# Two chunk-state products side by side, and products recorded in bundles, in a planned encoder kernel

## The chip, the cores and the metric

The kernel runs on one core of one Trainium2 chip. What is measured is the time of one execution on the device, in microseconds (us). Three runs of the kernel before took 2340.8, 2342.04 and 2342.53 us; the median, 2342.04 us, is the time before.

## What is computed

The reference is an encoder of two layers over 512 tokens with 1024 features, all in float32. Each layer has three branches that read the same normed input and are merged by sigmoid gates: an attention over a neighbourhood of rows and columns (16 heads), a dilated attention in three groups of 8 heads with windows of 128, 512 and 2048 tokens, and a state-space branch that runs over the tokens in both directions. After the merge come an output projection and a gated embedding. Most of the work is in the projections `h @ w_in`, 16,432 columns wide.

The change touches the state-space branch in its arithmetic. There the 512 tokens are cut in 4 chunks of 128. Per group of heads and direction the reference computes (shortened):

```python
decay_to_end = jnp.exp(a_cum[..., -1:] - a_cum)
chunk_states = jnp.einsum('bclgn,bghcl,bclghp->cbghpn', bc, decay_to_end, xdt)
def carry_state(state, inp):
    st, dec = inp
    return state * dec[..., None, None] + st, state
_, entering = lax.scan(carry_state, init, (chunk_states, chunk_decay))
y_off = jnp.einsum('bclgn,cbghpn,bghcl->bclghp', cc, entering, jnp.exp(a_cum))
```

`bc` is the same in both directions; the scaled inputs differ. Forward, the states of chunks 0, 1 and 2 are needed (the last one enters no chunk), backward those of 3, 2 and 1.

## The kernel before

The kernel is not written in the order in which it runs. `Emit` calls every operation of both layers on a `Recorder`, which makes a node of each call (`add`, line 222) with its engine, its tiles and its predecessors: nodes that wrote what it reads, and so on. A tile in PSUM counts as one whole: every product into it is behind the one before it. Then `schedule` (line 279) plays the program on a model of the chip and writes out an order for each queue; on the chip every engine works off its own order, and a semaphore wait stands where a tile was written by another engine.

In the model an instruction has a price (`cost`, line 151), a transfer has one too, and results come free for other engines after a fixed latency. An engine that is free takes among the nodes whose inputs are ready the one of lowest rank. The rank is the place in the program, less 300 for the weight splits, less 60 for what reads PSUM. For TensorE each product has a mode: `wide` (float32r, the projections), `full` (4-byte products and transposes), `pair` (4-byte products with 64 output rows, where two heads stand side by side in the array), `half` (64 input rows). TensorE's choice stays in the present mode if, among up to 12 older nodes of other modes, there is one of the present mode within 60 places of the oldest. A change of mode is priced at 45 ns between wide and full and 95 ns otherwise.

Around this the program has these parts. `proj` (line 490) makes one block of 128 output columns: a weight block of 128x1024 is fetched on SP's queue, split by ScalarE into a high part (whi) and by VectorE into a low part (wlo), and 24 float32r products of 512 columns go to a PSUM tile pj (3 buffers). `ssm_pair` (line 800) handles two heads of the state-space branch, 12 times a layer: a convolution, chunk states into tiles sc (2 buffers), a recurrence on VectorE over three states for each direction, decay factors from transfers on GpSimd's queue (af, ab, eb), the product inside a chunk into the tile av (1 buffer), 8 products with heads 0 and 1 in turn, and the product with the entering states (yo, in sc). The dilated branch (`dil_half`, line 911) and the neighbourhood branch (`na_unit`, line 1095) each run scores (`scores`, `dil_pair`, into sc), softmax on VectorE and ScalarE, transposes (`turn`, line 1004, into tr) and the products with the values into av, again head 0 and head 1 in turn: 8 products in a group of the dilated branch with dilation, 16 in the near one and in the neighbourhood branch. `stack` (line 1131) makes high and low halves of queries and keys for the score products. The stages run in the order N0 S0 N1 S1 N2 S2, half of the output product, S3 N3, its other half, the gate, D0 D1 (dilated), and the merges; the planner overlaps neighbours in this order.

Each 4-byte product shows in the trace as two TensorE records, each transpose and each float32r product as one. All operations are recorded at one line (270), so that tiles and not lines tell them apart: pj projections, av products with values, tr transposes, sc scores and states.

Of the kernel before, what the change touches and what calls it, by code (L numbers as in the profile page):

```python
# [119 lines left out]

class Node:
    __slots__ = ("i", "eng", "method", "args", "kw", "tiles", "pred", "succ", "cost", "dma", "table", "fetch", "issue",
                 "npred", "ready", "done", "rank", "split", "drain", "mode")


LATENCY = {"PE": {"PE": 0.0, "*": 197.0}, "ACT": {"ACT": 63.0, "PE": 271.0, "POOL": 159.0, "*": 142.0},
# [1 line left out]
           "POOL": {"POOL": 102.0, "PE": 203.0, "*": 75.0}, "SP": {"*": 0.0}}  # L128
RELEASE = {"tensor": 197.0, "scalar": 271.0, "vector": 287.0, "gpsimd": 203.0}
QUEUE = {"sync": "SP", "scalar": "ACT", "gpsimd": "POOL", "vector": "DVE", "tensor": "PE"}  # L130


FLEX = {"either": ("vector", "gpsimd")}
# [17 lines left out]
def cost(n, eng):  # L151

    args = list(n.args) + list(n.kw.values())
    lazy = [v for v in args if isinstance(v, Lazy)]
    out = n.kw.get("out", n.kw.get("out_", n.args[0] if n.args else None))
    if not isinstance(out, Lazy):
        out = lazy[0]
    free = 1
    for o, k, s in out.box[1:]:
        free *= k  # L160
    if n.dma:
        return 4.0 * free * out.box[0][1] / 360.0
    if eng == "tensor":
        if n.method == "transpose":
            return 107.0
        if lazy[1].base.dtype == F32R:
            return 111.0 if lazy[1].box[0][1] == 64 else 0.418 * free + 13.5
        if out.box[0][1] <= 64:
            return 54.0 if out.box[0][0] >= 64 else 1.72 * max(free, 64)
        if lazy[1].box[0][1] == 64:  # L170
            return 136.0
        return 1.75 * max(free, 124)
    psum = any(v.base.pool.space == "PSUM" for v in lazy)
    ptr = sum(1 for v in lazy if v.box[1:] and all(k == 1 for o, k, s in v.box[1:]))
    if eng == "scalar":
        return (51 if psum else 93) + 93 * ptr + free / 1.2
    if eng == "vector":
        if n.method == "reciprocal":
            return 64 + 6.27 * free
        if n.method == "tensor_tensor_reduce":  # L180
            ptr = 0
        half = n.method in ("tensor_copy", "tensor_scalar", "memset") and not psum
        return (64 + 61 * ptr + (free / 2 if half else free)) / 0.96
    if n.method == "memset":
        return 60 + free / 1.2
    if n.method == "tensor_copy":
        return 280 + free / 1.2
    if n.method == "tensor_mul" and any(v.box[-1][1] == 1 for v in lazy):
        return 1000.0
    return 160 + 2.08 * free  # L190


class Recorder:
# [28 lines left out]
    def add(self, eng, method, args, kw):  # L222
        n = Node()
        n.i, n.eng, n.method, n.args, n.kw = len(self.nodes), eng, method, args, kw
        n.dma = method == "dma_start"
        n.split = False
        n.drain = eng != "tensor" and any(isinstance(v, Lazy) and v.base.pool.space == "PSUM"
                                          for v in list(args) + list(kw.values()))
        n.fetch = n.dma and isinstance(kw["out"], Lazy) and kw["out"].base.pool.space != "DRAM"
# [32 lines left out]
        self.nodes.append(n)  # L262
        return n

    def emit(self, tc):
        order = self.schedule()
        with tc.manual_schedule():
            for n in order:
                f = lambda v: v.real() if isinstance(v, Lazy) else v
                getattr(getattr(self.real, n.eng), n.method)(*[f(a) for a in n.args],  # L270
                                                             **{k: f(v) for k, v in n.kw.items()})

    EARLY = 300
    DRAIN = 60
    STAY, NEAR = 12, 60
    WINDOW = 2500
    AHEAD = 600

    def schedule(self):
# [16 lines left out]
        self.first, self.placed = first, set()  # L296
        for n in nodes:
            n.npred = len(n.pred)
            n.rank = n.i - (self.EARLY if n.split else self.DRAIN if n.drain else 0)
            n.ready = 0.0  # L300
            for m in n.pred:
                m.succ.append(n)
            for t, wr in n.tiles.items():
                t.left += 1
# [13 lines left out]
        while len(order) < len(nodes):  # L318
# [3 lines left out]
            for q in avail:  # L322
# [50 lines left out]
                else:  # L373
# [2 lines left out]
                        table = n.table  # L376
                        c += 1283.0
                    if q == "tensor":
                        c += 0.0 if n.mode == mode else 45.0 if {n.mode, mode} == {"wide", "full"} else 95.0
                        mode = n.mode  # L380
                    clock[q] = n.done = now + c
                    busy[q] += c
# [50 lines left out]
class Emit:  # L433
# [366 lines left out]
    def ssm_pair(self, p, C, cbf, cbb, Bt):  # L800
# [2 lines left out]
        zz = self.silu2(self.proj("w_in", ZC + 128 * p))  # L803
        xt = self.transpose4(xs)

        ent = []
        for d in range(2):
            r0 = 32 * d + 2 * p
            c0 = d
            cx = self.t((128, 3, 2, 64), nm="cx")  # L810
            nc.vector.tensor_mul(cx, xt[:, c0:c0 + 3].rearrange("p c (h e) -> p c h e", h=2),
                                 self.cfT[:, c0:c0 + 3, r0:r0 + 2].unsqueeze(3).to_broadcast([128, 3, 2, 64]))
            st = self.ps("sc", (128, 3, 128))
            for c in range(3):
                nc.tensor.matmul(st[:, c], Bt[:, c0 + c], cx[:, c].rearrange("p h e -> p (h e)"),
                                 start=True, stop=True)
            E = self.t((128, 3, 128), nm="ent")
            order = (0, 1, 2) if d == 0 else (2, 1, 0)
            nc.scalar.copy(E[:, order[0]], st[:, order[0]])
            for a, b in zip(order, order[1:]):  # L820
                for h in range(2):
                    hs = slice(64 * h, 64 * h + 64)
                    nc.vector.scalar_tensor_tensor(E[:, b, hs], E[:, a, hs],
                                                   self.dec[:, r0 + h, c0 + b:c0 + b + 1],
                                                   st[:, b, hs], ALU.mult, ALU.add)
            ent.append(E)

        zs = []
        for h in range(2):
# [15 lines left out]
            nc.vector.tensor_mul(z, z, af)  # L845
            zs.append(z)
        yd = self.ps("av", (128, 4, 128))
        for c in range(4):
            for h in range(2):
                nc.tensor.matmul(yd[64 * h:64 * h + 64, c], xt[:, c, 64 * h:64 * h + 64], zs[h][:, c],  # L850
                                 start=True, stop=True)
        y = self.t(nm="y")
        nc.vector.scalar_tensor_tensor(y, xs, self.vec(V_DS + p), yd.rearrange("p c l -> p (c l)"),
                                       ALU.mult, ALU.add)
# [56 lines left out]
    def dil_half(self, hf):  # L911
# [8 lines left out]
        for pp in range(2):  # L920
            P = 2 * hf + pp
            for g in range(3):
# [3 lines left out]
                    qs, ks, kl = self.stack(q, k)  # L926
                pts = self.dil_near(qs, ks, kl, st, 2 * pp) if g == 0 else self.dil_pair(g, q, k, st, 2 * pp)
                av = self.ps("av", (128, 4, 128))
                for i in range(4):
                    terms = [((i + c + 3) % 4, i // 2, 2 * (i % 2) + c) for c in range(2)] if g == 0 else [(i, 0, i)]  # L930
                    for c, (t, b, u) in enumerate(terms):
                        for h in range(2):
                            vo = 128 * pp + 64 * h
                            nc.tensor.matmul(av[64 * h:64 * h + 64, i], val(g, t)[:, vo:vo + 64],
                                             pts[h][b][:, u], start=c == 0, stop=c == len(terms) - 1)
                o = self.t(nm="o")
                if g == 0:
                    nc.scalar.copy(o, av.rearrange("p t m -> p (t m)"))
# [54 lines left out]
    def scores(self, pair, q, k, kl):  # L993

        nc = self.nc
        sc = [self.ps("sc", (128, 2, 256)) for _ in range(2)]
        for h in range(2):
            for ii in range(2):
                nc.tensor.matmul(sc[h][:, ii], q(h, pair, ii), k(h, pair, ii), start=ii == 0, stop=False)
            for ii in range(2):  # L1000
                nc.tensor.matmul(sc[h][:, ii], q(h, pair, ii), kl(h, pair, ii), start=False, stop=ii == 1)
        return sc

    def turn(self, p):
        nc = self.nc
        tr = self.ps("tr", (128, 4, 128))
        pv = p.rearrange("p a (c k) -> p (a c) k", k=128) if p.shape[1] == 2 else p
        for c in range(4):
            nc.tensor.transpose(tr[:, c], pv[:, c], self.ident)
        pt = self.t((128, 4, 128), nm="pt")  # L1010
        nc.scalar.copy(pt, tr)
        return pt
# [36 lines left out]
    def dil_pair(self, g, q, k, st, hl):  # L1049
        nc = self.nc  # L1050
        sc = [self.ps("sc", (128, 4, 128)) for _ in range(2)]
        for t in range(4):
            for h in range(2):
                hs = slice(64 * h, 64 * h + 64)
                nc.tensor.matmul(sc[h][:, t], q[hs, t], k[hs, t], start=True, stop=True)
        pts = []
        for h in range(2):
            mx, dn = self.stats(st, g, hl + h)
# [36 lines left out]
    def na_unit(self, u):  # L1095
# [13 lines left out]
        for pp in range(2):  # L1109
# [4 lines left out]
            zz = self.silu2(self.proj("w_in", GA + 128 * P))  # L1114
            pts = self.na_pair(qs, ks, kl, P)
            av = self.ps("av", (128, 4, 128))
            for j in range(4):
                for c in range(2):
                    for h in range(2):
                        vo = 128 * pp + 64 * h  # L1120
                        nc.tensor.matmul(av[64 * h:64 * h + 64, j], V[self.BAND[j] + 16 * c][:, vo:vo + 64],
                                         pts[h][j // 2][:, 2 * (j % 2) + c], start=c == 0, stop=c == 1)
            y = self.t(nm="y")
            nc.vector.tensor_mul(y.rearrange("p (r j c) -> p j r c", j=4, c=16),
                                 av.rearrange("p j (r c) -> p j r c", c=16),
# [5 lines left out]
    def stack(self, qp, kp, scale=1.0, perm=lambda t: t, view=lambda t: t, eng=None):  # L1131
# [5 lines left out]
        qs = [self.t(dtype=F32R, nm="qs") for _ in range(2)]  # L1137
        ks = [self.t(dtype=F32R, nm="ks") for _ in range(2)]
        kl = self.keylow[self.nkey % 2]
        self.nkey += 1  # L1140
        for h in range(2):
            a, b = own[h], own[1 - h]
# [8 lines left out]
        for h in range(2):  # L1151
# [2 lines left out]
                nc.scalar.copy(ks[h][b], kp[a])  # L1154
            else:
                nc.scalar.activation(ks[h][b], kp[a], AF.Copy, scale=scale)
        return qs, ks, kl

    BAND = (0, 8, 24, 32)
# [259 lines left out]
```

## Time and profile before

| | |
|---|---|
| median of three runs | 2342.04 us |
| profiled execution | 2345.19 us |
| its span, first to last instruction | 2342.9 us |
| TensorE, busy | 2282.3 us (97%) |
| VectorE, busy | 1643.4 us (70%) |
| ScalarE, busy | 1112.8 us (47%) |
| GpSimd, busy | 219.1 us (9%) |
| mean granted clock of TensorE | 0.991 |
| moved by transfers | 272.69 MB, 116 GB/s over the span |

A busy time is the union of the spans of an engine's instructions. Matmuls are pipelined: one starts before the one before it has ended, and its end is modelled. What a product costs in a stream is therefore read from the start of one to the start of another, on the timeline.

### The profile page before, as it was taken

Reading aid. Unit: us, or ns where it says so; the run is one execution under the profiler, and the core shown is the slowest. Engines: PE = TensorE matmul, PEld = TensorE weight load, DVE = VectorE, ACT = ScalarE, POOL = GpSimd, SP = SyncE. Lnnn points to the kernel's source line nnn. Section 1 sums busy time; section 2 is a strip of 40 time slices with the busy share of each in tenths; the row PEclk is TensorE's granted clock in tenths of the full one; section 3 lists DMA queues with packets and bytes.
Section 4 is the critical chain, followed back from the end, with each engine's and each line's share of the span. In section 5 each row is a group of like instructions: output and inputs, shape, how many; then the busy total and the mean of one; then the engine's idle time right before and its main releaser. Section 6 shows DMA issues by size and latency. Waiting matters only on the chain. (4 is left out here: it accounts for less than half of the span.)

```text
span 2342.9 us, 32733 instructions
## 1 busy us (share of the span) xinstructions
PE 2282.3 (97%) x12096; PEld 1880.5 (80%) x12096; DVE 1643.4 (70%) x3227; ACT 1112.8 (47%) x2132; POOL 219.1 (9%) x384
## 2 busy tenths in 40 slices
PE   7899999999999999999998999999999999999998
PEld 6688888888887877888877888888789778778888
DVE  6699979796356577635677998797943666665367
ACT  5456455444345456324465463644532554562245
POOL 1401020010000100200013110210100001011000
PEclk8999999999999999999999999999999999999999
DMA  5734262432221321533256333534322213225324
GB/s 217 212 99 152 85 186 77 144 99 91 90 90 64 91 81 64 172 128 112 105 179 185 110 128 106 161 101 133 107 84 99 72 67 106 73 66 171 111 103 135
DMA packets 109326, 272.69 MB, mean 116 GB/s; under 512 B 39360, under 2 KB 41888, under 8 KB 109168
## 3 DMA queue, kind: packets, MB, share of 16 engines
q1 hardware_dynamic: 56464, 189.73, 23.7%
q0 software_dynamic: 50400, 76.69, 11.6%
q10 hardware_dynamic: 2304, 4.20, 0.5%
q8 instruction: 95, 1.56, 0.3%
q14 instruction: 63, 0.52, 0.1%
HBM read 257.08 MB, written 13.21 MB: 115 GB/s over the span
## 5 line engine op out<-in xcount | busy, mean ns | idle before, releaser
L270 ACT CAST whi<-raw 128x1024 fp32r<-128x1024 f32 (+2 forms) x360 | 368.3, 1023 | 696.8 <-PE pj L270 511.4
L270 PE MATMUL pj<-hl,whi 128*128 128x512 f32 x1744 | 693.3, 398 | 2.1 <-DVE hl L270 2.1
L270 PE MATMUL pj<-hh,whi 128*128 128x512 f32 x1744 | 693.0, 397 | 1.5 <-ACT hh L270 1.5
L270 PE MATMUL pj<-hh,wlo 128*128 128x512 f32 x1728 | 687.4, 398 | 0.4 <-DVE wlo L270 0.4
L270 DVE TENSOR_TENSOR wlo<-raw,whi 128x1024 fp32r<-128x1024 f32 (+2 forms) x358 | 426.3, 1191 | 349.4 <-ACT whi L270 345.9
L270 PEld LDWEIGHTS pj<-hl,whi 128*128 128x128 f32 x1744 | 330.3, 189 | 70.7 <-issue 5.7
L270 PEld LDWEIGHTS pj<-hh,whi 128*128 128x128 f32 x1744 | 330.5, 190 | 66.5 <-issue 2.4
L270 PEld LDWEIGHTS pj<-hh,wlo 128*128 128x128 f32 x1728 | 326.2, 189 | 71.2 <-issue 9.3
L270 PE MATMUL pj<-yh,whi 128*128 128x512 f32 (+1 forms) x576 | 211.9, 368 | 0.0
L270 PE MATMUL pj<-yh,wlo 128*128 128x512 f32 (+1 forms) x576 | 211.5, 367 | 0.0
L270 PE MATMUL pj<-yl,whi 128*128 128x512 f32 (+1 forms) x576 | 211.0, 366 | 0.0
L270 PEld LDWEIGHTS pj<-yh,wlo 128*128 128x128 f32 x576 | 108.7, 189 | 18.0 <-issue 0.7
L270 PEld LDWEIGHTS pj<-yh,whi 128*128 128x128 f32 x576 | 108.6, 189 | 17.5 <-issue 0.7
L270 PEld LDWEIGHTS pj<-yl,whi 128*128 128x128 f32 x576 | 108.7, 189 | 17.1
L270 DVE SCALAR_TENSOR_TENSOR cv<-cx,cwh,cv 128x510 f32<-128x510 f32 (+1 forms) x160 | 119.5, 747 | 2.3 <-ACT cv L270 0.3
L270 ACT ACTIVATE p<-p,nm 128x128 f32<-128x128 f32 (+2 forms) x192 | 80.2, 420 | 33.6 <-DVE nm L270 33.6
L270 PE MATMUL pj<-whi,hh 128*128 128x512 f32 (+1 forms) x256 | 88.7, 348 | 2.0 <-ACT v L270 2.0
L270 PE MATMUL pj<-whi,hl 128*128 128x512 f32 (+1 forms) x256 | 87.6, 342 | 0.8 <-DVE hl L270 0.8
L270 PE MATMUL pj<-wlo,hh 128*128 128x512 f32 (+1 forms) x256 | 87.8, 343 | 0.0
L270 ACT ACTIVATE np<-np,nnm 128x256 f32<-128x256 f32 x128 | 63.7, 499 | 48.9 <-DVE nnm L270 48.9
L270 ACT COPY pt<-tr 128x512 f32<-128x512 f32 x128 | 71.2, 579 | 26.3 <-PE tr L270 25.2
L270 POOL DMA_DIRECT2D af<-acd x48 | 28.4, 591 | 483.3 <-DVE y L270 224.5
(215 smaller groups left out, 3577.9 us busy)
## 6 DMA issues: line engine op xcount, KB each, us to landing
raw<-wt SPq DMA_DIRECT2D x322, 512.0 KB, 3.2
nb<-nab POOLq DMA_DIRECT2D x32, 384.0 KB, 5.4
af<-acd POOLq DMA_DIRECT2D x48, 256.0 KB, 4.8
ab<-acd POOLq DMA_DIRECT2D x48, 256.0 KB, 5.5
raw<-wt SPq DMA_DIRECT2D x32, 384.0 KB, 2.9
eb<-ead POOLq DMA_DIRECT2D x48, 192.0 KB, 8.5
vw<-vd POOLq DMA_DIRECT2D x56, 128.0 KB, 5.0
f<-fd POOLq DMA_DIRECT2D x24, 256.0 KB, 11.1
```

The costliest lines, as they stand in the source:

```text
L270: getattr(getattr(self.real, n.eng), n.method)(*[f(a) for a in n.args], **{k: f(v) for k, v in n.kw.items()})
```

## The change

Six things are changed. The states of both directions are made chunk by chunk: the scaled inputs that share a chunk's weights stand side by side (256 columns for chunks 1 and 2, 128 for 0 and 3), in two PSUM tiles that both recurrences read. A new `bundle` puts all predecessors of a group of products in front of the group's first one; it is called for the av groups, the scores, the transposes and the dilated pairs. A change of mode is priced by a table with an entry for each direction. GpSimd's transfers are priced at 1.6 times, broadcasts by `to_broadcast` at 4 times. The nodes of `stack` are ranked 200 places earlier. A 4-byte product is priced as before.

```diff
+CHANGE = {("wide", "full"): 39.0, ("full", "wide"): 0.0, ("pair", "wide"): 202.0, ("wide", "pair"): 78.0,
+          ("full", "pair"): 108.0, ("pair", "full"): 140.0, ("half", "wide"): 187.0, ("wide", "half"): 53.0}
...
     if n.dma:
-        return 4.0 * free * out.box[0][1] / 360.0
+        c = 4.0 * free * out.box[0][1] / 360.0
+        if eng != "gpsimd":
+            return c
+        ops = [m for m, a, k in n.kw["in_"].ops] if isinstance(n.kw["in_"], Lazy) else []
+        return 4.0 * c if "to_broadcast" in ops else 1.6 * c
...
+    def bundle(self, start):
+
+        group = self.nodes[start:]
+        for eng in {n.eng for n in group}:
+            own = [n for n in group if n.eng == eng]
+            for n in own[1:]:
+                for m in n.pred:
+                    if m.i < start:
+                        own[0].pred[m] = True
...
-            n.rank = n.i - (self.EARLY if n.split else self.DRAIN if n.drain else 0)
+            n.rank = n.i - (self.EARLY if n.split else self.STACK if n.stack else self.DRAIN if n.drain else 0)
...
-                        c += 0.0 if n.mode == mode else 45.0 if {n.mode, mode} == {"wide", "full"} else 95.0
+                        c += 0.0 if n.mode == mode else CHANGE.get((mode, n.mode), 100.0)
...
+        r = (2 * p, 32 + 2 * p)
+        own = lambda lo, n, d: self.cfT[:, lo:lo + n, r[d]:r[d] + 2].unsqueeze(3).to_broadcast([128, n, 2, 64])
+        four = lambda t: t.rearrange("p c (h e) -> p c h e", h=2)
+        ca, cb2 = self.t((128, 3, 128), nm="cx"), self.t((128, 3, 128), nm="cx")
+        nc.vector.tensor_mul(four(ca[:, 0:2]), four(xt[:, 0:2]), own(0, 2, 0))
+        nc.vector.tensor_mul(four(ca[:, 2:3]), four(xt[:, 1:2]), own(1, 1, 1))
+        nc.vector.tensor_mul(four(cb2[:, 0:1]), four(xt[:, 2:3]), own(2, 1, 0))
+        nc.vector.tensor_mul(four(cb2[:, 1:3]), four(xt[:, 2:4]), own(2, 2, 1))
+        sa, sb = self.ps("sc", (128, 3, 128)), self.ps("sc", (128, 3, 128))
+        for st, cx, c, lo, hi in ((sa, ca, 0, 0, 1), (sa, ca, 1, 1, 3), (sb, cb2, 2, 0, 2), (sb, cb2, 3, 2, 3)):
+            nc.tensor.matmul(st[:, lo:hi], Bt[:, c], cx[:, lo:hi], start=True, stop=True)
         ent = []
-        for d in range(2):
-            r0 = 32 * d + 2 * p
-            c0 = d
-            cx = self.t((128, 3, 2, 64), nm="cx")
-            nc.vector.tensor_mul(cx, xt[:, c0:c0 + 3].rearrange("p c (h e) -> p c h e", h=2),
-                                 self.cfT[:, c0:c0 + 3, r0:r0 + 2].unsqueeze(3).to_broadcast([128, 3, 2, 64]))
-            st = self.ps("sc", (128, 3, 128))
-            for c in range(3):
-                nc.tensor.matmul(st[:, c], Bt[:, c0 + c], cx[:, c].rearrange("p h e -> p (h e)"),
-                                 start=True, stop=True)
+        for d, steps in enumerate((((0, 0, sa[:, 0]), (1, 1, sa[:, 1]), (2, 2, sb[:, 0])),
+                                   ((2, 3, sb[:, 2]), (1, 2, sb[:, 1]), (0, 1, sa[:, 2])))):
             E = self.t((128, 3, 128), nm="ent")
...
         yd = self.ps("av", (128, 4, 128))
+        mark = len(nc.nodes)
         for c in range(4):
             for h in range(2):
                 nc.tensor.matmul(yd[64 * h:64 * h + 64, c], xt[:, c, 64 * h:64 * h + 64], zs[h][:, c],
                                  start=True, stop=True)
+        nc.bundle(mark)
...
+        mark = len(nc.nodes)
         for c in range(4):
             nc.tensor.transpose(tr[:, c], pv[:, c], self.ident)
+        nc.bundle(mark)
...
+        for n in nc.nodes[mark:]:
+            n.stack = True
         return qs, ks, kl
```

The same two lines `mark` and `bundle` stand around the av products of `dil_half` and `na_unit` and around the score products of `scores` and `dil_pair`. The recurrence steps and the copies of the first states are the same in number and size.

## Rows read from the trace of the kernel before

**Rows 1.** The page: engine busy us, share, instructions; VectorE's tenths in 40 slices.
```profile
PE 2282.3 (97%) x12096; PEld 1880.5 (80%) x12096; DVE 1643.4 (70%) x3227; ACT 1112.8 (47%) x2132; POOL 219.1 (9%) x384
...
DVE  6699979796356577635677998797943666665367
```
**Rows 2.** Timeline of TensorE, long products: start us, duration us, operation, tiles, shape.
```profile
999.62 0.39 PE L270 MATMUL pj<-hl,whi 128*128 128x512 f32 x1
...
1008.91 0.39 PE L270 MATMUL pj<-hh,whi 128*128 128x512 f32 x1
```
**Rows 3.** Timeline of TensorE, a split av group, state-space; last visit of 14.
```profile
167.13 0.40 PE L270 MATMUL pj<-hl,whi 128*128 128x512 f32 x1
167.45 0.43 PE L270 MATMUL av<-z,tT 128*64 128x128 f32 x2
...
168.16 0.40 PE L270 MATMUL pj<-hh,whi 128*128 128x512 f32 x1
...
171.39 0.39 PE L270 MATMUL pj<-hh,wlo 128*128 128x512 f32 x1
171.71 1.09 PE L270 MATMUL av<-z,tT 128*64 128x128 f32 x14
...
173.06 0.40 PE L270 MATMUL pj<-hl,whi 128*128 128x512 f32 x1
...
1680.61 1.09 PE L270 MATMUL av<-z,tT 128*64 128x128 f32 x14
```
**Rows 4.** Timeline of TensorE, unbroken av visits of 16 and of 32 records.
```profile
338.33 0.40 PE L270 MATMUL pj<-hh,whi 128*128 128x512 f32 x1
338.65 1.09 PE L270 MATMUL av<-pt,vw 128*64 128x128 f32 x16
...
340.01 0.39 PE L270 MATMUL pj<-hh,wlo 128*128 128x512 f32 x1
...
559.84 1.97 PE L270 MATMUL av<-pt,vw 128*64 128x128 f32 x32
...
562.08 0.40 PE L270 MATMUL pj<-yl,whi 128*128 128x512 f32 x1
```
**Rows 5.** Timeline of TensorE, dilated part: the first and last av visit of two.
```profile
691.14 0.43 PE L270 MATMUL av<-pt,v 128*64 128x128 f32 x2
...
2085.58 0.43 PE L270 MATMUL av<-pt,v 128*64 128x128 f32 x2 [0.67 <-ACT pt L270]
```
**Rows 6.** Timeline of TensorE, a single softmax transpose between long products.
```profile
705.55 0.40 PE L270 MATMUL pj<-hl,whi 128*128 128x512 f32 x1
705.81 0.33 PE L270 MATMUL tr<-consts,p 128*128 128x128 f32 x1
...
706.21 0.40 PE L270 MATMUL pj<-hh,whi 128*128 128x512 f32 x1
```
**Rows 7.** Timeline of TensorE, chunk states, and products with one column.
```profile
161.94 1.50 PE L270 MATMUL sc<-cx,tT 128*128 128x128 f32 x12
...
163.51 0.40 PE L270 MATMUL pj<-hh,whi 128*128 128x512 f32 x1
...
596.14 0.95 PE L270 MATMUL sc<-consts,sq 128*128 128x1 f32 x8
...
597.28 0.40 PE L270 MATMUL pj<-hh,wlo 128*128 128x512 f32 x1
```
**Rows 8.** VectorE's groups by form: count, then busy us, mean ns, idle before.
```profile
L270 DVE TENSOR_TENSOR cx<-tT,cfT 128x384 f32<-128x384 f32 x48 | 24.5, 551 | 0.0
...
L270 DVE TENSOR_TENSOR gth<-pj,r 128x256 f32<-128x256 f32 x18 | 7.4, 421 | 2.7 <-PE pj L270 2.7
```
**Rows 9.** Waits of TensorE: us in total, times, longest us.
```profile
PE tr L270 <- DVE np L270: 14.0, 2, 7.1
```
**Rows 10.** One slice: length, busy us of PE, PEld, DVE, ACT, POOL, clock, DMA.
```profile
468.60:527.20 58.60, 57.91 (x325) 47.19 (x325) 58.24 (x113) 27.71 (x45) 6.34 (x11) 1.00 0.32 99
```

More of the change, by code (lines that the diff above doesn't have):

```diff
@@ L122 @@
     __slots__ = ("i", "eng", "method", "args", "kw", "tiles", "pred", "succ", "cost", "dma", "table", "fetch", "issue",
-                 "npred", "ready", "done", "rank", "split", "drain", "mode")
+                 "npred", "ready", "done", "rank", "split", "stack", "drain", "mode")
 LATENCY = {"PE": {"PE": 0.0, "*": 197.0}, "ACT": {"ACT": 63.0, "PE": 271.0, "POOL": 159.0, "*": 142.0},
@@ L225, in add @@
         n.dma = method == "dma_start"
-        n.split = False
+        n.split = n.stack = False
         n.drain = eng != "tensor" and any(isinstance(v, Lazy) and v.base.pool.space == "PSUM"
@@ L274 @@
     DRAIN = 60
+    STACK = 200
     STAY, NEAR = 12, 60
@@ L817, in ssm_pair @@
             E = self.t((128, 3, 128), nm="ent")
-            order = (0, 1, 2) if d == 0 else (2, 1, 0)
-            nc.scalar.copy(E[:, order[0]], st[:, order[0]])
-            for a, b in zip(order, order[1:]):
+            nc.scalar.copy(E[:, steps[0][0]], steps[0][2])
+            for (i, _, _), (j, c, st) in zip(steps, steps[1:]):
                 for h in range(2):
                     hs = slice(64 * h, 64 * h + 64)
-                    nc.vector.scalar_tensor_tensor(E[:, b, hs], E[:, a, hs],
-                                                   self.dec[:, r0 + h, c0 + b:c0 + b + 1],
-                                                   st[:, b, hs], ALU.mult, ALU.add)
+                    nc.vector.scalar_tensor_tensor(E[:, j, hs], E[:, i, hs], self.dec[:, r[d] + h, c:c + 1],
+                                                   st[:, hs], ALU.mult, ALU.add)
@@ L996, in scores @@
         sc = [self.ps("sc", (128, 2, 256)) for _ in range(2)]
+        mark = len(nc.nodes)
         for h in range(2):
@@ L1001, in scores @@
                 nc.tensor.matmul(sc[h][:, ii], q(h, pair, ii), kl(h, pair, ii), start=False, stop=ii == 1)
+        nc.bundle(mark)
         return sc
@@ L1007, in turn @@
         pv = p.rearrange("p a (c k) -> p (a c) k", k=128) if p.shape[1] == 2 else p
+        mark = len(nc.nodes)
         for c in range(4):
             nc.tensor.transpose(tr[:, c], pv[:, c], self.ident)
+        nc.bundle(mark)
         pt = self.t((128, 4, 128), nm="pt")
@@ L1051, in dil_pair @@
         sc = [self.ps("sc", (128, 4, 128)) for _ in range(2)]
+        mark = len(nc.nodes)
         for t in range(4):
@@ L1055, in dil_pair @@
                 nc.tensor.matmul(sc[h][:, t], q[hs, t], k[hs, t], start=True, stop=True)
+        nc.bundle(mark)
         pts = []
@@ L1116, in na_unit @@
             av = self.ps("av", (128, 4, 128))
+            mark = len(nc.nodes)
             for j in range(4):
@@ L1122, in na_unit @@
                                          pts[h][j // 2][:, 2 * (j % 2) + c], start=c == 0, stop=c == 1)
+            nc.bundle(mark)
             y = self.t(nm="y")
@@ L1139, in stack @@
         kl = self.keylow[self.nkey % 2]
+        mark = len(nc.nodes)
         self.nkey += 1
```

## The prediction

> **What bounds the kernel now.** I read the page's engine table first: TensorE is busy 2282.3 of 2342.9 us, VectorE 1643.4 [rows 1]. Matmul ends are modelled, so a busy TensorE may still lose time between products; I therefore went to its timeline and measured from start to start. In an undisturbed stream of long products (float32r, 128x512) 41 of them take 1008.91 - 999.62 = 9.29 us, 0.227 us each [rows 2]. Where another kind of product comes between two long ones, I take the time from the start of the last long one before it to the start of the second one after it, less 2 x 0.227 us. That is the true price of the visit, with what the neighbours lose.
>
> A visit of the half-width kind (outputs 64 rows wide, tile av) prices so. Two records, that is one product: 168.16 - 167.13 - 0.454 = 0.576 us. Fourteen records: 173.06 - 171.39 - 0.454 = 1.216 us [rows 3]. Sixteen: 340.01 - 338.33 - 0.454 = 1.226 us. Thirty-two: 562.08 - 559.84 - 0.227 = 2.01 us, with 0.09 us for the entry 2.10 us [rows 4]. So sixteen more records cost 0.88 us, and a visit as such 1.226 - 0.88 = 0.35 us. Fourteen cost what sixteen do: the lone product at the start of a group takes as long as the pair of products (one for each head, side by side) that it is torn from. The reader is to see that a group split into 2 + 14 costs 0.576 us more than a whole one, and ends no sooner after its last input.
>
> And groups are split nearly always. The timeline holds 149 av visits for 64 groups: all 24 of the state-space part stand as 2 + 14 [rows 3]; the dilated part has 32 of 2 and 32 of 14 records for 24 groups [rows 5]; the neighbourhood part has 37 visits (15 of 16 as in [rows 4], 10 of 2, 7 of 14, 3 of 30, 2 of 32) for 16 groups of 32. The planner issues the first product once head 0 is ready, and then goes back to long products.
>
> **The change part by part.** The sum is made against the profiled execution, 2345.19 us (span 2342.9), which lies 3.15 us above the median of 2342.04.
>
> *Bundles on av.* No product is added or taken away. The first product of a group is planned behind all inputs, the others follow in a chain. Visits go from 149 to 64. State-space: 24 x 0.576 = 13.8 us. Dilated groups of 16: 16 x 0.576 = 9.2 us. Dilated groups of 32, now 2, 14, 2, 14: 8 x (2 x 0.576 + 2 x 1.216 - 2.10) = 11.9 us. Neighbourhood: some 43 to 45 us of visits against 16 x 2.10 = 33.6 us, I take 10 us. Together 45 us, from a timeline in which TensorE has hardly any idle time, so it lies on the path. The bound below is that the visits between other kinds are cheaper; at the bare 0.35 us a visit 85 of them make 30 us. Only the groups of 32 end later after their last input, by 0.88 us; their reader (an ACT copy or a VectorE product) has its next user one projection later.
>
> *Bundles on transposes.* The softmax transposes of the dilated part (4 to a group, 64 groups) stand in 144 visits, 96 of them single. A single one costs 706.21 - 705.55 - 0.454 = 0.206 us [rows 6]; in a run a record of this size costs 0.112 us [rows 7]. 80 visits fewer x 0.094 = 7.5 us at most; many single ones sit beside other 4-byte products, where no visit is closed, so I take 5 us, with 0 as the low end. The first three transposes of a group now wait for the fourth exponential, and the copy behind them comes some 0.3 us later; TensorE has long products meanwhile. The bundles on scores and on the dilated pairs change no kind of product: nothing.
>
> *Chunk states.* Per pair 6 products (12 records) become 4, two with 128 and two with 256 columns. Twelve records take 163.51 - 161.94 - 0.227 = 1.343 us, 0.112 each [rows 7]. Records of 256 columns do not occur in this type. One bound: the time is all streaming, then a 256-column record costs 0.219 to 0.224 us and nothing is gained. The other: the time is all weight load, then it costs 0.112 and each pair gains 4 x 0.112 = 0.448 us, 24 pairs 10.75 us. A record with one column costs 0.114 us [rows 7], which allows the second; but the av products have weights 64 columns wide, and two side by side still take 0.88 us / 8 = 0.110 us a record at 128 columns [rows 4], which speaks for streaming. I take 0.5 us. VectorE gets 2 x 0.421 + 2 x 0.29 us (128 columns, by the slope from 256 to 384) in place of 2 x 0.551 us [rows 8], +0.32 us a pair, 7.7 us in all. Both sc buffers are held until both recurrences end, about 1.1 us longer (four steps); scores, cb and the y products of the next step wait for these buffers, and would cost 24 x 1.1 = 26 us if TensorE had nothing else; it has projections, so 0.
>
> [...]
>
> *Planner's prices and ranks* (switch costs, GpSimd transfers at 1.6 or 4 times, q/k stacks 200 places earlier). They change the order only. The largest idle stretches they could remove are two waits of 7.1 us for np, 14.0 us in all [rows 9]; they could as well make two more. I take 0, with 14 to either side.
>
> *What is late next.* Where VectorE is full, TensorE can't run ahead: 58.24 of 58.6 us from 468.6 on [rows 10]. Nine of the 40 slices have VectorE at 90% or more [rows 1], all in the two stretches where 24 us of the av gain falls; I take back a third of that, 8 us, the added multiplies included.
>
> Sum: 45 + 5 + 0.5 - 8 = 42.5 us. 2345.2 - 42.5 = 2302.7, on the scale of the median 2299.5.
>
> **The rivals.** (1) VectorE and the new order take half: 22 to 28 us remain, about 2317. For it: the full slices and 7.7 us more VectorE work; against it: its share is 70% [rows 1]. (2) Slower: TensorE runs out of ready work in front of the bundles. Already now it stands idle 0.67 us in front of an av product whose head 0 had not come [rows 5]; a bundle waits for head 1 as well. If each of the 128 bundles (64 av, 64 dilated transposes) met 0.64 us, that is 82 us of idle against 50.5 us, 2372. It decides from 50.5 / 128 = 0.39 us a bundle. Against it: in the state-space part TensorE is hardly idle. (3) Weight load bounds the 4-byte products: all as forecast, and 10.3 us more gained, 2289. (4) The bundles don't hold: after the first product the planner still prefers a long one more than 60 places older. Then only the 0.5 us of the states remains, 2341.5. Against it: every 14 in the timeline is unbroken.
>
> **How the numbers follow.** Forecast 0.61, rival 1 0.20, rival 2 0.07, rival 3 0.06, rival 4 0.06. The forecast's own range is 2285 to 2316 (bare visit price, 14 us of order to either side). 8 in 10 times I expect 2280 to 2332: rival 1 and 3 are in, 2 and 4 out. A difference under 0.2% (4.7 us) counts as none. Faster: 0.61 + 0.20 + 0.06 = 0.87; same 0.05 (rival 4, without its tail); slower 0.08.
>
> **What would show it.** After: av visits of 16 and 32 records alone, 64 of them; single transposes nearly gone; TensorE's union of busy time some 40 us lower with idle time within 15 us of now; state records of 256 columns near 0.22 us. Records of 0.112 us would prove the weight-load view. Idle of 0.5 us in front of most bundles would prove rival 2; VectorE over 95% with TensorE waiting for wlo or np rival 1; visits of 2 and 14 still there rival 4.

## The result and the profile after

The changed kernel takes 2298.76 us (median of four runs, 2297.84 to 2302.36) against 2342.28 us; the ratio is 0.9817, interval 0.98 to 0.9834. The forecast was 2299.5 us. The profiled execution took 2299.15 us, its span is 2296.0 us.

The page of the changed kernel, the engines' busy us, share and instructions, and VectorE's tenths in 40 slices, answers to [rows 1]:

```profile
PE 2233.6 (97%) x12000; PEld 1858.5 (81%) x12000; DVE 1645.1 (72%) x3275; ACT 1115.6 (49%) x2132; POOL 218.0 (9%) x384
...
DVE  6799979796357676635678998897943677664367
```

TensorE's busy time has fallen by 48.7 us and the span by 46.9; the idle time hardly moved (2342.9 - 2282.3 = 60.6 us before, 62.4 us now). So the time came out of what TensorE does, not out of its waiting. Where, the timeline shows (start us, duration us, operation): a state-space av group, one of the neighbourhood branch, and four softmax transposes of the dilated stage, each between long products.

```profile
93.70 0.39 PE L288 MATMUL pj<-hl,whi 128*128 128x512 f32 x1
94.02 1.97 PE L288 MATMUL av<-pt,vw 128*64 128x128 f32 x32
...
96.25 0.40 PE L288 MATMUL pj<-hh,whi 128*128 128x512 f32 x1
...
160.97 0.39 PE L288 MATMUL pj<-hl,whi 128*128 128x512 f32 x1
161.29 1.09 PE L288 MATMUL av<-z,tT 128*64 128x128 f32 x16
...
162.65 0.40 PE L288 MATMUL pj<-hh,whi 128*128 128x512 f32 x1
...
680.75 0.39 PE L288 MATMUL pj<-hl,whi 128*128 128x512 f32 x1
680.99 0.60 PE L288 MATMUL tr<-consts,p 128*128 128x128 f32 x4
...
681.65 0.39 PE L288 MATMUL pj<-hh,whi 128*128 128x512 f32 x1
```

All 64 av groups stand unbroken now: 40 visits of 16 records and 24 of 32, in place of 149. A visit of 16 costs 162.65 - 160.97 - 0.454 = 1.226 us, one of 32 96.25 - 93.70 - 0.454 = 2.10 us, as in [rows 4]. The softmax transposes of the dilated part stand four by four in 64 visits (144 before), and four cost 681.65 - 680.75 - 0.454 = 0.446 us.

The chunk states, on the same timeline and in TensorE's groups by form (count, then busy us and mean ns of one), answer to [rows 7]:

```profile
152.15 0.40 PE L288 MATMUL pj<-hh,wlo 128*128 128x512 f32 x1
152.44 1.63 PE L288 MATMUL sc<-cx,tT 128*128 128x128 f32 x8
...
154.13 0.39 PE L288 MATMUL pj<-hl,whi 128*128 128x512 f32 x1
```
```profile
L288 PE MATMUL sc<-cx,tT 128*128 128x256 f32 x96 | 26.8, 395 | 0.0
...
L288 PE MATMUL sc<-cx,tT 128*128 128x128 f32 x96 | 19.5, 284 | 0.9 <-DVE cx L288 0.9
```

Eight records take 154.13 - 152.15 - 0.454 = 1.526 us; of 21 unbroken visits between long products 18 have no reported idle time; these lie between 1.31 and 1.54 us, median 1.45. Twelve took 1.34 us before. From start to start a 256-column record costs 0.215 to 0.219 us, about twice the 0.109 to 0.112 us of 128 columns: the streaming bound of the forecast, not the weight-load bound. What comes on top are steps of 0.075 us, where the first record of a product stands 0.184 or 0.291 us from the next in place of 0.109 or 0.216. They are waits for VectorE, too short to be reported as idle: where a 256-column product starts 0.147 us behind the end of the multiply that it reads, the step is 0.291 us, at 0.178 us behind it 0.260 us, at 0.30 us 0.216 us. In e3 below, eight unbroken visits whose multiplies had ended some 0.30 us or more before their products show no long step and take 1.31 to 1.32 us.

TensorE's waits, with total us, times and longest us:

```profile
PE sc L288 <- DVE rq L288: 10.4, 16, 1.2
...
PE tr L288 <- ACT p L288: 5.3, 4, 1.3
...
PE tr L288 <- DVE np L288: 2.9, 5, 1.0
```

The two long waits for np, 14.0 us [rows 9], have shrunk to 2.9 us; in their place the dilated stages wait 10.4 us for rq (3.9 us before). The 5.3 us for p are spent ahead of the transposes of the softmax statistics, not of the bundled ones.

The two waits for np cost more than their own length, because the granted clock of TensorE fell in them from 1.00 to 0.50. A stretch of the kernel before (start:end, length, busy us of PE, PEld, DVE, ACT, POOL, granted clock, DMA share, GB/s) and TensorE's timeline in it:

```profile
97.00:103.83 6.83, 4.71 (x24) 3.89 (x26) 5.51 (x15) 2.20 (x4) 4.22 (x8) 0.50 0.80 188
```
```profile
99.12 1.94 PE L270 MATMUL tr<-consts,np 128*128 128x128 f32 x8 [6.83 <-DVE np L270]
...
101.29 0.63 PE L270 MATMUL pj<-hl,whi 128*128 128x512 f32 x1
101.72 0.63 PE L270 MATMUL pj<-hh,wlo 128*128 128x512 f32 x1
```

From 96.95 to 103.78 us, at the end of the wait and for 4.7 us behind it, the granted clock is 0.50, and long products start 0.43 us apart in place of 0.227. Apart from the start and the end of the span, the kernel before has three such stretches (at the two waits for np and at one of 2.3 us for ks), the changed kernel none, and its mean granted clock is 0.995 in place of 0.991. Against the same steps at full clock the three cost 5 us; this is an estimate from the trace, without the idle time.

To see where in the kernel the gain fell, I cut the span of each run at five points of TensorE's timeline: the first softmax transpose of each dilated stage and the last av product of it, and the start of layer 1. us, with TensorE's idle time before its products in brackets (53.8 us in all before, 55.6 after):

| stage | before | after | bundles alone (e1) | best (e12) |
|---|---|---|---|---|
| start, neighbourhood and state-space, layer 0 | 689.7 (23.4) | 675.7 (20.9) | 682.4 (26.9) | 674.9 (19.6) |
| dilated, layer 0 | 249.2 (8.0) | 240.7 (12.1) | 241.7 (13.3) | 231.4 (2.6) |
| merges to layer 1 | 235.0 (0.4) | 233.2 (0.0) | 233.8 (0.0) | 232.1 (0.0) |
| neighbourhood and state-space, layer 1 | 670.5 (11.7) | 657.8 (9.1) | 664.2 (12.7) | 655.1 (7.1) |
| dilated, layer 1 | 247.7 (7.6) | 239.3 (10.9) | 239.9 (12.3) | 231.2 (2.5) |
| rest | 250.6 (2.7) | 249.3 (2.6) | 249.7 (3.1) | 248.9 (3.0) |

### The profile page after: what moved, and what is told of

It is laid out like the page before. It is cut to its first block, busy times and chain, and to the rows that moved or that the text cites. A ratio compares the mean times of both kernels' runs of the same rounds, so it can differ in the third digit from the quotient of the medians.

```text
span 2296.0 us, 32560 instructions
## 1 busy us (share of the span) xinstructions
PE 2233.6 (97%) x12000; PEld 1858.5 (81%) x12000; DVE 1645.1 (72%) x3275; ACT 1115.6 (49%) x2132; POOL 218.0 (9%) x384
## 3 DMA queue, kind: packets, MB, share of 16 engines
q8 instruction: 94, 1.54, 0.3%
## 5 line engine op out<-in xcount | busy, mean ns | idle before, releaser
L288 ACT ACTIVATE p<-p,nm 128x128 f32<-128x128 f32 (+2 forms) x192 | 80.3, 421 | 55.6 <-DVE nm L288 55.3
L288 DVE CUSTOM_DVE_ANT_0 p<-sc,consts 128x128 f32<-128x128 f32 (+2 forms) x192 | 49.3, 318 | 18.0 <-PE sc L288 18.0
```

## The experiments

Theory A: the gain is the price of TensorE's visits to half-width products. Its rival, theory B: the planner's new prices and ranks order the work better, and the bundles matter little. Between sets of runs the time of the same kernel differs by some us (medians of 2342.3 to 2345.7 for the one before), so ratios to the runs of the kernel before on the same chip are compared. 0.001 is 2.3 us, an interval is about 0.0015 to either side.

| run | what it is | us | ratio |
|---|---|---|---|
| after | the changed kernel | 2298.76 | 0.9817 |
| e1 | before + bundles | 2314.22 | 0.9878 |
| e2 | after, without bundles | 2339.36 | 0.9985 |
| e3 | before + new states | 2346.43 | 1.001 |
| e4 | after, old states | 2299.32 | 0.9811 |
| e5 | before + bundles + prices | 2298.46 | 0.9805 |
| e6 | before + bundles + stack rank | 2308.12 | 0.9849 |
| e7 | after, bundles on av alone | 2299.53 | 0.9813 |
| e8 | e4 + strided price | 2283.08 | 0.9737 |
| e9 | after, state-space av not bundled | 2306.72 | 0.9848 |
| e10 | after, spare VectorE multiplies | 2317.15 | 0.9891 |
| e11 | before + bundles + GpSimd prices | 2293.47 | 0.9793 |
| e12 | e8 + price of the half shift | 2275.72 | 0.9718 |

**e1, the bundles alone.** The kernel before with `bundle` and its calls.

> The kernel before with the bundles alone: old chunk states, old prices and ranks. Theory A (the gain is TensorE's visits to half-width products, 149 of them made 64): 64 visits, av price down by 46 us, time 2290 to 2303 us. Theory B (prices and earlier stacks order the work better, the bundles only help): under half of the gain, 2320 us or more.

0.9878 (0.9863 to 0.9893): 28.6 us, two thirds of the gain, between the two expectations. The 64 visits are there, and TensorE's av price without idle falls from 132.8 to 97.3 us (each visit from the start of the record before it to the start of the one behind it, less one step of the former). But TensorE waits longer. The waits of e1:

```profile
PE sc L284 <- DVE rq L284: 12.7, 16, 1.3
PE tr L284 <- DVE np L284: 12.3, 3, 6.3
PE sc L284 <- DVE qs L284: 8.2, 2, 4.1
```

The np waits stay, and rq and qs waits join them (3.9 us and 1.4 us before): idle between products grows from 53.8 to 68.3 us, the sums of the brackets in the table above; 10.0 us of the growth lie in the two dilated stages. The clock is at 0.50 in five stretches, behind waits for np, qs and ks, and by the same estimate as above they cost 10 us.

**e2, the rest without the bundles.**

```diff
         group = self.nodes[start:]
+        return
```

> The changed kernel with bundles that do nothing: new states, prices and ranks stay. Theory A: the groups are split as before (about 149 visits), time 2335 to 2350 us. Theory B: 2320 us or less.

0.9985 (0.9976 to 0.9994): 3.5 us gained. The av visits are 164. Theory A holds and B falls as a theory of the whole; but e1 and e2 add up to 32 us, not to 43. A part of the difference is that without bundles the new order tears more groups than the old one (149 visits): the av visits cost TensorE 5.9 us more without idle than before. e5, e6 and e11 ask which part of the prices is worth something behind the bundles.

**e3 and e4, the chunk states.** e3 puts the new states into the kernel before, e4 the old ones into the changed kernel.

> The kernel before with the new chunk states alone. Streaming theory: records of 256 columns stay at 0.215 us or more, the visit of 8 records costs 1.32 us without waits and 1.45 us with them against 1.34 us for 12 before; 0 to 5 us slower than before, 2342 to 2347 us. Weight-load theory: 10 us faster, 2332 us.

> The changed kernel with the old chunk states (six products, two multiplies a pair); bundles, prices and ranks stay. If the new states cost what the trace after shows (1.44 us a visit against 1.34, three visits split): 2 to 4 us faster than the changed kernel, 2294 to 2297 us. If they are free: 2298 to 2299 us.

e3: 1.001 (1.0001 to 1.002), 2.3 us slower. e4: 0.9811 (0.9798 to 0.9825), not to be told from the changed kernel. The part that gives the change its name is worth nothing, or costs 2 us. The 10 us of the weight-load view are refuted by e3's time and by the 0.215 us in the trace.

**e5, e6, e11: which price.** Old states in all three. e5 has bundles and all prices, e6 bundles and the stack rank, e11 bundles and this alone:

```diff
-        return 4.0 * free * out.box[0][1] / 360.0
+        c = 4.0 * free * out.box[0][1] / 360.0
+        if eng != "gpsimd":
+            return c
+        ops = [m for m, a, k in n.kw["in_"].ops] if isinstance(n.kw["in_"], Lazy) else []
+        return 4.0 * c if "to_broadcast" in ops else 1.6 * c
```

> The kernel before with bundles and the new prices, without the earlier rank of the q/k stacks and without the new chunk states. Theory P (the dearer GpSimd transfers keep VectorE from queueing up in front of a decay row that has not landed, which is what the two waits of 7 us for np were): no wait for np over 3 us, 2298 to 2306 us, 8 us or more below the bundles alone (2314). Theory S (the earlier stacks do it): 2311 to 2316 us with the np waits still there.

> The kernel before with bundles and the earlier rank of the stacks, old prices, old chunk states. Theory P: the np waits of 5 to 7 us stay, 2308 to 2316 us. Theory S: they go, 2298 to 2306 us.

> The kernel before with bundles and the dearer GpSimd transfers alone; mode changes at the old prices, no earlier stacks, old chunk states. If the transfers' price is what the prices are worth: 2297 to 2303 us, as with both (2298.5). If the table of mode changes carries it: 2309 to 2315 us, as the bundles alone (2314).

e11 is at 0.9793 (0.9779 to 0.9806): the dearer GpSimd transfers are worth 20 us on top of the bundles, and they alone make all that the other edits make together or more, faster than expected. Between the profiled runs of e1 and e11 TensorE's idle time falls by 17.2 us, and the stretches at the lower clock from five to two, some 5 us more by the estimate. The table of mode changes adds nothing (e5, 0.9805, no faster than e11). The earlier stacks bring some 7 us alone (e6 against e1; the intervals touch) and nothing behind the prices (e4 against e5). Theory P was right on the price but not in saying that only the price removes the np waits: in e6 they are down to 1.3 us too, and it is at 0.9849.

How a price of transfers becomes waiting of TensorE is on VectorE's timeline of the kernel before, just ahead of the first np wait (start us, duration us, operation, in brackets the idle time and what ended it):

```profile
92.23 0.17 DVE L270 RECIPROCAL ndn<-ndn 128x4 f32<-128x4 f32 x1
97.81 0.69 DVE L270 TENSOR_TENSOR ab<-ab,acT 128x512 f32<-128x512 f32 x1 [5.41 <-DMA ab<-acd]
98.42 1.34 DVE L270 TENSOR_SCALAR np<-np,ndn 128x256 f32<-128x256 f32 x4
```

The planner thought that the decay row ab had landed, and put its subtraction in front of the scaling of np. VectorE took the two in that order: it stood 5.41 us for the transfer, np was scaled behind it, and TensorE stood 7 us for np. In the changed kernel the np scalings at this place run ahead of the subtraction. VectorE's waits for ab in the kernel before, e1 and e6 (total us, times, longest us):

```profile
DVE ab L270 <- DMA ab<-acd: 14.6, 3, 7.6
...
DVE ab L284 <- DMA ab<-acd: 13.1, 4, 5.6
...
DVE ab L284 <- DMA ab<-acd: 7.0, 3, 3.5
```

With the dearer transfers they go: 1.1 us in e5, none in e11.

**e7, the transposes.** The changed kernel, `bundle` at the av groups alone.

> The changed kernel with bundles on the av groups alone; transposes, scores and dilated pairs are free to be split. If the transposes' visits cost the 0.09 us each that the trace of before shows (144 visits against 64): 3 to 7 us slower than the changed kernel, 2302 to 2306 us. Rival: the wait for the fourth exponential costs the dilated stage as much as the visits save: 2296 to 2300 us.

0.9813 (0.9798 to 0.9827), the same as with all bundles. The softmax transposes of the dilated part are torn into 160 visits again (64 in the changed kernel), but the dilated stages of e7 take 240.6 and 240.7 us with 10.6 and 10.7 us idle, against 240.7 and 239.3 with 12.1 and 10.9. So in these stages the torn visits cost 3.1 us without idle, and 1.7 us less idle time stands against it. That is little for 96 more visits, because 68 transposes stand one by one with a single long product between two: there a pair of transpose and long product takes 0.364 us on average, which leaves 0.137 us for the transpose, near the 0.112 us in a row and not the 0.206 us of the one in [rows 6]. Waits for exponentials are not the reason: ahead of these transposes TensorE waits 7.2 us in e7 and under 1 us in the changed kernel.

**e9, splits put back.** The changed kernel without `nc.bundle(mark)` behind the 24 state-space av groups.

> The changed kernel without the bundle around the 24 state-space av groups; all other bundles stay. Switch theory: 24 visits of 2 and 24 of 14 records come back, 88 av visits in all, +24 x 0.576 = 13.8 us, 2309 to 2315 us. If the split only shifts waiting that exists anyway: 2297 to 2304 us.

0.9848 (0.9835 to 0.9862), some 7 us slower than the changed kernel, half of the 13.8 and between the two expectations. One of the torn groups, on TensorE's timeline:

```profile
175.92 0.40 PE L288 MATMUL pj<-hh,whi 128*128 128x512 f32 x1
176.31 0.40 PE L288 MATMUL av<-z,tT 128*64 128x128 f32 x2
...
176.98 0.39 PE L288 MATMUL pj<-hh,wlo 128*128 128x512 f32 x1
```

It costs 176.98 - 175.92 - 0.454 = 0.606 us here, and over the kernel the av visits, 88 now, cost TensorE 11.0 us more without idle (105.1 against 94.1), and 20 more of them lead into long products, which lose 0.11 us each behind a visit: 13.2 us. The price was right. But TensorE's idle time is 2.6 us shorter: a part of what a visit costs in these stretches is time that TensorE would have waited. The rest of the difference, some 3 us, was not traced.

**e10, VectorE's slack.** The changed kernel with two more multiplies a pair:

```diff
+        spare = self.t((128, 3, 128), nm="cy"), self.t((128, 3, 128), nm="cy")
+        for i in range(2):
+            nc.vector.tensor_mul(four(spare[i]), four(xt[:, i:i + 3]), own(i, 3, i))
```

> The changed kernel with two spare multiplies of 128x384 for each pair, whose results nobody reads: 48 x 0.465 us = 22 us more on VectorE, all of it in the two state-space stretches. If VectorE bounds part of these stretches (rival 1, and the 8 us taken back in the forecast): 5 to 15 us slower, 2304 to 2314 us. If it has slack there: 2297 to 2302 us.

0.9891 (0.9877 to 0.9904): 17 us slower, beyond the range for a VectorE that bounds only a part. The page, two of TensorE's waits, which the changed kernel does not have at this size (0.7 us for z, none for eb), and one of VectorE's:

```profile
PE 2240.3 (97%) x12000; PEld 1861.3 (81%) x12000; DVE 1666.6 (72%) x3323; ACT 1115.1 (48%) x2132; POOL 217.5 (9%) x384
```
```profile
PE av L288 <- DVE z L288: 5.6, 4, 1.6
...
PE sc L288 <- DVE eb L288: 4.6, 2, 2.4
...
DVE eb L288 <- DMA eb<-ead: 4.2, 2, 2.2
```

21.5 us more busy time on an engine with a share of 72% cost 17 us. Between the profiled runs 9.0 us are idle time, and some 5 us by the estimate a lower clock, at 0.50 in three stretches that the changed kernel does not have. So work added to VectorE in the state-space stretches reaches TensorE. Not all of it is lack of time on VectorE: in front of the two waits for eb VectorE itself stood 4.2 us for the transfer of eb, the same in-order wait as for ab. How much comes from the other order that the planner writes with the extra work, these runs don't separate.

**e8 and e12, a version that beats both.** The changed kernel leaves 10.4 us of waits for rq. TensorE and VectorE around one of them (VectorE first):

```profile
828.85 1.18 DVE L288 TENSOR_TENSOR rq<-rq,consts 128x512 f32<-128x512 f32 x1
829.93 1.10 DVE L288 TENSOR_TENSOR rs<-rs,consts 128x512 f32<-128x512 f32 x1
830.93 1.23 DVE L288 TENSOR_TENSOR wlo<-raw,whi 128x1024 fp32r<-128x1024 f32 x1
832.07 0.69 DVE L288 TENSOR_TENSOR rq<-rq,rs 128x512 f32<-128x512 f32 x1
```
```profile
832.81 1.16 PE L288 MATMUL sc<-rq,rq 64*128 64x128 f32 x16 [1.05 <-DVE rq L288]
```

The two multiplies read the rotary tables with a step of four elements. They take 1.08 and 1.00 us from start to start where an ordinary multiply takes 0.60, and the planner prices both kinds alike; so it believes there is time for a weight split in between. In the group without dilation the same instruction reads the same table without a step: in the kernel before the 16 multiplies rq<-rq,consts there take 0.61 us from start to start (827.37 to 827.98 us), the 32 with the step 0.98 to 1.02 us. Why the step costs 0.4 us no trace shows; a step of four is the only one that occurs here. e8 is e4 with

```diff
+    apart = 400.0 if any(v.base.pool.space != "PSUM" and any(m == "rearrange" and "(m t)" in a[0] for m, a, k in v.ops)
+                         for v in lazy) else 0.0
+    if apart and eng in ("scalar", "vector"):
+        return apart + (free / 1.2 + 93 if eng == "scalar" else (64 + free) / 0.96)
```

> The changed kernel with the old chunk states, and rotary multiplies and copies that read or write every fourth element priced 0.4 us dearer on VectorE and ScalarE, as the trace shows them (1.00 us from start to start against 0.60). If the 10 us that TensorE waits for rq in the dilated stages come from that price, most of them go: 2288 to 2295 us. If these waits have another cause: 2297 to 2302 us.

0.9737 (0.9724 to 0.975), 2283.08 us, beyond the expectation: the waits for rq fall to 1.3 us, and the dilated stages to 234.1 and 231.6 us. The edit prices copies with such a step as well; what either kind is worth alone was not run. e12 adds 100 ns for copies and subtractions between the two halves of the partitions:

> The fastest version so far (old chunk states, strided operations priced dearer, 2283 us), and besides 0.1 us more for the copies and subtractions of the q/k stacks that move 64 rows to the other half. TensorE still waits 4.8 us for ks there, two times. If that price is the cause: 2278 to 2282 us; if not: 2282 to 2286 us.

0.9718 (0.9705 to 0.9732), 2275.72 us, faster than expected; the intervals of e8 and e12 overlap a little. The largest waits of e12, behind the one for the first weights at the start:

```profile
PE sc L294 <- DVE std L294: 3.8, 2, 2.6
PE pj L294 <- DVE hl L294: 2.9, 2, 2.1
...
PE sc L294 <- ACT ks L294: 1.9, 2, 1.0
```

By the page's counts it issues the same instructions on TensorE, VectorE, ScalarE and GpSimd as the kernel before, in another order, and is 66 us faster. Beyond the start and the end of the span its clock is never at 0.50.

## Why the prediction was right, and where two errors met

*Visits to av: right in kind, number and price.* 149 became 64 with no group torn. The price without idle went from 132.8 to 94.1 us, 38.7 us; with 63 exits into long products fewer (121 to 58) at 0.11 us that is 45.6 us, 45 was forecast. Not every visit's price is a gain, as e9 shows: in the state-space part half of it.

*Rival 2 did not come, but the dilated stages lose.* In front of and inside the 128 bundles TensorE stands idle 1.8 us in all, 0.014 us each where rival 2 needed 0.39 (its price adds up to 2373.5, not 2372). But the forecast left the dilated stages without a loss, and their idle time grew by 4.1 and 3.3 us, most of it for rq. It is not a matter of the bundle around those scores: in e7, without it, the wait for rq is 10.9 us. e8 shows the cause, strided operations priced too low. Of the 21 us that were to come off their av visits, 16.9 us arrived (8.5 and 8.4 us in the table).

*Transposes: sized 5 us, measured nothing* (e7). The price was read from a lone transpose with long products on both sides. Of the 58 single ones between long products before, 50 alternate with them, and there a pair of both takes 0.378 us on average, 0.15 us for the transpose.

*States: sized at a gain of 0.5 us, measured 0 to 2 us of loss* (e3, e4). The streaming view was right (0.215 to 0.219 us a record), rival 3, whose 10.3 us are the 10.75 of the weight-load bound less 0.5, did not come, and a visit that waits for nothing is 0.03 us cheaper than before, 0.7 us for 24. The short waits for the multiplies, now four in place of two, were not in the sum. VectorE's extra work was put too high: 7.7 us by mean durations, where one instruction starts before the one before it has ended (a multiply of 256 columns lasts 0.419 us, and the next starts 0.335 us behind its start); its busy time rose by 3.8 us in e3.

*Prices and ranks: taken as 0, worth 14 us behind the bundles in the changed kernel* (e1 against it), and 17 to 20 us with the old states (e5, e11). This is the term that was sized worst: 14 us was the bound that the forecast gave it, from the two np waits, and it took the middle. It did not count the lower clock behind such waits, and not the waits that the bundles would bring. In the kernel before, VectorE's wait for the transfer of ab [5.41 <-DMA ab<-acd] stands just ahead of the np scaling; the price of that transfer was in the change.

*The brake taken off, 8 us, was too small and in the wrong place.* It was meant for the state-space stretches. With the bundles alone TensorE's idle time grew by 14.5 us, 10.0 us of it in the dilated stages, where the forecast had no brake, and some 5 us more went with the clock. e10 shows that VectorE has little to spare in the state-space stretches; that can be the cause of the smaller part only.

The forecast thus gave the bundles 45 + 5 - 8 = 42 us and the rest of the change 0.5 us; the runs gave 28.6 and 14.3 us. The mechanism and the price of the visits were right, but that the total came out within 1 us of 2299.5 is luck: errors of 13.4 and 13.8 us cancelled.

## What to carry to other kernels

Where a bound engine changes between kinds of work, price a visit from the start of the last product before to the second one after, count the visits, and look for groups that are begun before all their inputs are there: the lone first product was no faster than a pair (a visit of 14 records took 1.216 us, one of 16 took 1.226) and ended nothing sooner. In a planned kernel the planner's price for a single class of instruction (transfers, strided reads) can be worth as much as an edit of the arithmetic; the place to find it is an in-order engine that stands in front of the engine which the waits name. An engine at 72% over the span can have little slack in the stage where it counts (21.5 us more on VectorE cost 17 us in e10); add work to it there before calling it hidden. The price of a visit holds for the neighbours that it was read between: a lone transpose between long products took 0.206 us, one that alternates with them 0.137. And look at the granted clock behind a long wait: in the kernel before it was 0.50 behind three of them, some 5 us in all by the estimate beyond their own length.

## What the runs showed of the hardware

In the kernel before, two 4-byte products with 64 output rows each, side by side, take as long as one alone (0.22 us for either, out of the visits of 14 and of 16 records, 1.216 and 1.226 us). A 4-byte record costs 0.109 to 0.112 us at 128 columns and 0.114 us at one column (before), and 0.215 to 0.219 us at 256 (the changed kernel). The product behind a long one that follows a half-width visit starts 0.11 us late (0.337 us from start to start in place of 0.227). Such a visit costs 0.35 us beyond its records; a visit of twelve full-width 4-byte records costs 1.34 us, which is twelve times 0.112 and nothing more. In three waits of the kernel before, of 2.3, 6.8 and 7.1 us, the granted clock of TensorE fell from 1.00 to 0.50; at 0.50 long products start 0.427 us apart. VectorE multiplies with a step of four elements in one operand cost 1.0 us where unit steps cost 0.60 to 0.61 us (128x512).
